# The gates' ring and the sums of quarters of h.T get memory of their own beside the projections of queries and keys, and the first sum is kept

## The chip, the core and the metric

The kernel runs as one program on one core of a Trainium2 chip. A core has a matrix engine (PE in the profile), three engines for elementwise work (DVE, ACT, POOL), a queue engine (SP) and 16 DMA engines, which share one on-chip memory; each engine works through its own instructions in a fixed order and waits for others by semaphores. The metric is the device time of one execution in microseconds. The kernel before was run three times: 1585.13, 1587.35 and 1588.13 us, so the median is 1587.35 us.

## What is computed

One layer of a decoder trunk: a token mixer with three branches (a gated short convolution, a state space model called S5, and latent attention), and then a mixture of experts. Sequence and model width are 1024. The change touches the mixer's input projection and its gates:

```python
proj = h @ w_in                              # 1024 x 1024 times 1024 x (2016 + 3 x 1024)
(xc, gc, gb, u_ssm, c_q, c_kv, k_r,
 g_conv, g_ssm, g_attn) = jnp.split(proj, IN_SPLITS, axis=-1)
y_conv = (gb * causal_conv(gc * xc)) @ w_up_conv
y_ssm  = s5_branch(u_ssm, ...) @ w_up_ssm
y_attn = attention(rms_norm(c_q), rms_norm(c_kv), k_r, ...) @ w_up_attn
merged = sigmoid(g_conv) * y_conv + sigmoid(g_ssm) * y_ssm + sigmoid(g_attn) * y_attn
y = merged @ w_o
```

## The kernel before

All matrix products take f32 operands as two parts each, a high part and a low one (`split_into`, L117 to L129: the cast that makes the high part runs on ACT at L125, the subtraction that leaves the low part on DVE at L129), and three matmuls replace one (`mm3`, L139 to L142, low times high first). The modulated input stands transposed on chip as eight pairs of tiles hh[k], hl[k] of 128 x 1024 ("h.T"). A block of 128 columns of `w_in` is a tile of 512 KB that SP loads (named raw), that is split into whi and wlo, and that gives 48 matmuls of 128 x 512 (`proj`, two halves of eight steps of three).

The mixer (`mixer`, L279) goes through these steps, and this is also the order in which they are written: the S5 branch up to its outputs; the first five of the eight gates of attention (`gates_att(0, GA, ...)` with GA = 5: projection, a sigmoid on ACT at L1075, a DMA to memory that ACT issues at L468); `proj_qkv` (L877), which projects c_q, c_kv and k_r into the tile cq and then normalises it by rows in a long chain of small operations on DVE (square L921, split L129, ones-matmul ps_ss L924 and L925 on PE, scale L927, `rsqrt` L145 to L153 with a square root on ACT at L148 and a reciprocal on DVE at L149, result L930), after which ACT issues one DMA of cq to memory, called cqd (L932, 1.5 MB); the last three gates of attention; `moving_sums`; `pairs`; and then `branches` (L1079), the up-projections of the convolution and of S5.

`pairs` computes 28 more blocks of `w_in` two at a time with seven products in place of eight (Strassen's scheme in Winograd's form, `pair_proj`, L365). For this h.T is cut into four quarters, and three sums of quarters (t2, t3, t4) are made once in `moving_sums` (L342 adds the two parts of a tile back together, L348 makes the sums, t0h to t2l are their two parts). A fourth, t1 = b12 - b11, is formed on the way to t2. It is dropped there, and within the first pair `moving_sum1` (L356) forms it anew (L360, L361) and splits it into the right halves of hh[0..3] and hl[0..3], which nothing needs whole any more. The same sums of quarters are made of every pair of weight tiles (L375, L379), and split into wsa (tiles sah and sal), w22 and wsb.

The order on each engine is fixed when the program is built. A scheduler takes the operations as they are written and moves one ahead of another where its own estimate says that the engine would else wait; memory decides what may move, since a tile of a pool that lies where a closed pool lay waits for the last use of what was there. Two pools matter. `qkv` holds all tiles of `proj_qkv`, cq among them. `stp` is opened after `qkv` is closed, in the same memory, and holds the ring of four tiles that the gates, the convolution's inputs and its outputs go round in, the split sums t0h to t2l, eight spare tiles, and the split sums of weights. So the ring's tile for the sixth gate, and the first part t0h, wait for `proj_qkv` to end and in part for the landing of cqd.

## Time and profile before

| | |
|---|---|
| three runs | 1585.13, 1587.35, 1588.13 us, median 1587.35 us |
| the profiled execution | 1582.0 us, of which the trace's span is 1579.9 us |
| PE busy in the span | 1419.6 us, 90% |
| DVE busy | 1196.8 us, 76% |
| ACT busy | 733.4 us, 46% |
| mean granted TensorE clock, of full speed | 0.954 |

A profile is taken of one execution. Its rows are in microseconds from the span's start. "Idle before" is the time for which an engine had nothing to run ahead of an instruction, and the arrow names the operation whose end released it. In the text, a gate or a pair is named by its place in the list above: the norm chain is the end of `proj_qkv`, the transition is the step from the last pair to `branches`.

### The profile page before, as it was taken

What the parts mean: (1) busy time and instruction counts of PE and PEld (TensorE: products, weight loads), DVE (VectorE), ACT (ScalarE), POOL (GpSimd) and SP (SyncE); (2) the same over time, 40 slices, a digit from 0 to 9 for tenths busy, and PEclk for the clock granted to TensorE, in tenths of its full rate; (3) what the DMA queues carried; (4) which work ended last, traced back from release to release, by engine and by line L of the source; (5) the groups of instructions that cost most, each with busy time, mean ns of one, the idle gap of its engine ahead of it and who ended that gap; (6) DMA issues with size and microseconds to landing.
All of it is one profiled execution on the core that took longest, in us unless ns stands there. A gap on an engine that the chain in (4) does not pass through costs nothing.

```text
span 1579.9 us, 20183 instructions
## 1 busy us (share of the span) xinstructions
PE 1419.6 (90%) x6996; PEld 1144.4 (72%) x6996; DVE 1196.8 (76%) x1861; ACT 733.4 (46%) x1192; POOL 442.5 (28%) x599
## 2 busy tenths in 40 slices
PE   5599799479999999999799979999979999999983
PEld 3477678368888887887588867788967888888841
DVE  8464687898775547756587788778887999999948
ACT  6232112242223334130477763335424998999853
POOL 7999930000000000006211252400322322222216
PEclk9799999799999999999799998999999999999977
DMA  9232221132122248968200035634623777777643
GB/s 382 80 113 88 73 58 27 67 101 97 56 107 107 107 145 308 326 161 224 36 15 12 4 114 192 225 133 151 251 79 115 303 282 287 289 297 272 255 182 146
DMA packets 79940, 247.50 MB, mean 157 GB/s; under 512 B 18460, under 2 KB 29780, under 8 KB 71000
## 3 DMA queue, kind: packets, MB, share of 16 engines
q1 hardware_dynamic: 53670, 200.47, 36.0%
q10 hardware_dynamic: 15218, 24.68, 4.5%
q0 software_dynamic: 10944, 20.99, 4.2%
q8 instruction: 56, 0.92, 0.2%
q14 instruction: 52, 0.43, 0.1%
HBM read 252.74 MB, written 55.10 MB: 195 GB/s over the span
## 4 chain that ended last, share of the span: by engine, by line
PE 58%; DVE 14%; POOL 12%; DMA 7%; issue 5%; ACT 3%; ACTq 0%; DVEq 0%; POOLq 0%; SPq 0%
PE ps_mm L140 9%; PE ps_mm L141 9%; PE ps_mm L142 9%; DMA yd<-y,idx 4%; PE ps_up L140 3%; PE ps_h L140 3%; PE ps_h L142 3%; PE ps_h L141 3%; PE ps_up L141 3%; PE ps_up L142 3%; PE ps_O L1272 2%; PE ps_T L1258 2%; PE ps_y L140 1%; PE ps_y L142 1%; PE ps_tr L1635 1%
## 5 line engine op out<-in xcount | busy, mean ns | idle before, releaser
L1138 POOL TENSOR_TENSOR mg<-mg,sg 128x512 f32<-128x512 f32 x16 | 23.5, 1476 | 496.4 <-DVE sg L1137 492.8
L140 PE MATMUL ps_mm<-hh,wlo 128*128 128x512 f32 x304 | 123.5, 406 | 22.7 <-ACT sg L1075 15.6
L142 PE MATMUL ps_mm<-hh,whi 128*128 128x512 f32 x304 | 123.1, 405 | 0.0
L141 PE MATMUL ps_mm<-hl,whi 128*128 128x512 f32 x304 | 122.7, 404 | 0.0
L125 ACT CAST whi<-raw 128x1024 fp32r<-128x1024 f32 (+1 forms) x45 | 46.8, 1040 | 134.0 <-PE ps_up L142 65.2
L1672 POOL DMA_INDIRECT yd<-y,idx x33 | 46.5, 1409 | 170.4 <-ACT y L1671 98.4
L140 PEld LDWEIGHTS ps_mm<-hh,wlo 128*128 128x128 f32 x304 | 58.7, 193 | 37.6 <-ACT sg L1075 16.1
L129 DVE TENSOR_TENSOR qh<-wo,qh 128x1024 fp32r<-128x1024 f32 x66 | 80.5, 1220 | 5.1 <-ACT qh L125 5.1
L129 DVE TENSOR_TENSOR ql<-wo,ql 128x1024 fp32r<-128x1024 f32 x66 | 79.5, 1219 | 4.8 <-ACT ql L125 4.8
L129 DVE TENSOR_TENSOR wlo<-raw,whi 128x1024 fp32r<-128x1024 f32 x44 | 60.4, 1373 | 26.5 <-ACT whi L125 26.5
L125 ACT CAST qh<-wo 128x1024 fp32r<-128x1024 f32 x66 | 70.0, 1061 | 4.1 <-DMA wo<-exp 4.1
L142 PEld LDWEIGHTS ps_mm<-hh,whi 128*128 128x128 f32 x304 | 58.6, 193 | 14.9 <-issue 1.0
L141 PEld LDWEIGHTS ps_mm<-hl,whi 128*128 128x128 f32 x304 | 58.8, 193 | 13.7 <-issue 0.2
L125 ACT CAST ql<-wo 128x1024 fp32r<-128x1024 f32 x66 | 68.2, 1052 | 0.0
L125 ACT CAST xh<-ps_tr 128x512 fp32r<-128x512 f32 x66 | 39.5, 599 | 55.5 <-PE ps_tr L1635 55.4
L1610 POOL DMA_INDIRECT xg<-h2d,idx x35 | 37.1, 1061 | 77.1 <-PE ps_tr L1635 63.5
L1244 DVE TENSOR_REDUCE sm<-ps_S 128x1 f32<-128x256 f32 (+3 forms) x64 | 49.2, 770 | 10.8 <-PE ps_S L1241 10.1
L129 DVE TENSOR_TENSOR pl<-ps_T,ph 128x512 fp32r<-128x512 f32 (+1 forms) x80 | 45.9, 581 | 14.0 <-ACT ph L125 12.6
L140 PE MATMUL ps_up<-ah,wlo 128*128 128x512 f32 x128 | 50.6, 403 | 5.1 <-ACT ah L125 2.9
L391 DVE TENSOR_TENSOR sp<-ps_mm,sp 128x512 f32<-128x512 f32 x48 | 32.8, 686 | 28.0 <-PE ps_mm L142 27.8
L1245 ACT ACTIVATE p<-ps_S,sm 128x256 f32<-128x256 f32 (+3 forms) x64 | 48.5, 758 | 10.0 <-DVE sm L1244 9.4
L140 PE MATMUL ps_mm<-wo,ml 128*128 128x512 f32 x128 | 50.0, 398 | 2.8 <-DVE sg L1354 2.8
(727 smaller groups left out, 4733.2 us busy)
## 6 DMA issues: line engine op xcount, KB each, us to landing
wo<-exp SPq DMA_DIRECT2D x111, 1024.0 KB
raw<-w_in SPq DMA_DIRECT2D x43, 512.0 KB
adr<-w_ada SPq DMA_DIRECT2D x32, 512.0 KB
wada<-w_ada SPq DMA_DIRECT2D x16, 512.0 KB
fy<-yd SPq DMA_DIRECT2D x16, 512.0 KB
sga<-sg ACTq DMA_DIRECT2D x8, 512.0 KB
sgc<-sg ACTq DMA_DIRECT2D x8, 512.0 KB
sgs<-sg ACTq DMA_DIRECT2D x8, 512.0 KB
```

The lines of the kernel that those rows point to most:

```text
L125: nc.scalar.copy(out=hi, in_=src)
L129: e.tensor_tensor(out=lo, in0=src, in1=hi.bitcast(F32), op=ALU.subtract)
L140: mm(ps, wl, xh, start=first, stop=False)
L141: mm(ps, wh, xl, start=False, stop=False)
L142: mm(ps, wh, xh, start=False, stop=last)
L391: v.tensor_tensor(out=out, in0=p, in1=x, op=op)
L1244: v.tensor_reduce(out=sm[:], in_=x, axis=AX.XY if two else AX.X, op=ALU.max, negate=True)
L1245: act.activation(out=y, in_=x, func=AF.Exp, bias=sm[:], accum_out=d)
L1258: pe.transpose(pt[:, k2 * 256 + qi * 128:k2 * 256 + qi * 128 + 128], prob[h, c, qi][:, ks], self.ident[:])
L1272: pe.matmul(po[:, 0:256], vv[:, kt, h].rearrange("p z d -> p (z d)"), x[z], start=kt == 0 and z == 0, stop=kt == 2 * c + 1 and z == 1)
L1610: self.nc.gpsimd.indirect_dma_start(out=self.xg[b % 2][:], out_offset=None, in_=self.h2d[:], in_offset=bass.IndirectOffsetOnAxis(ap=self.i ...
L1672: nc.gpsimd.indirect_dma_start(out=self.yd[:], in_=y[:], in_offset=None, out_offset=bass.IndirectOffsetOnAxis(ap=self.idx[:, 1, b:b + 1], ...
```

## The change

The ring becomes a pool of its own with two tiles, opened before S5 (it takes the place of the pool `sgp`, which held two gate tiles during S5). A pool `tsp` with the split sums and four more tiles that keep t1 is opened before `qkv`. `stp` is still opened after `qkv` in its memory; it now holds the convolution's weights, four spare tiles, the split sums of weights, and two tiles of their own for the convolution's outputs and for gc. `moving_sum1` no longer forms t1, and only splits the kept tiles. The four tiles that kept t1 serve afterwards as the scratch of `evac_b`.

```diff
@@ -282,8 +282,9 @@
         with ExitStack() as hs:
             hpool = hs.enter_context(tc.tile_pool(name="hpool", bufs=1, reuse_waits="tile"))
             self.hslot = lambda n, k, x="", dt=F32R: hpool.tile([128, S], dt, name=f"{n}{k}{x}", tag=f"{n}{k}")
+            ring = hs.enter_context(tc.tile_pool(name="ring", bufs=1, reuse_waits="tile"))
+            self.ring = lambda n: ring.tile([128, S + 2], F32, name=n, tag="ring", bufs=2)
             with ExitStack() as st:
-                self.sgp = st.enter_context(tc.tile_pool(name="sgp", bufs=1, reuse_waits="tile"))
                 self.s5p = st.enter_context(tc.tile_pool(name="s5p", bufs=1, reuse_waits="tile"))
                 self.banks_for(mm=4, a=2, b=2)
                 self.uses = {"ss": "ab"}
@@ -307,13 +308,13 @@
                             prep.append(self.s5_prep(q + 2))
                     if self.stop == "s5":
                         return False
-                    self.gates_att(0, GA, lambda: self.sgp.tile([128, S], F32, name="sg", tag="sg", bufs=2))
+                    self.gates_att(0, GA)
+            self.tsp = hs.enter_context(tc.tile_pool(name="tsp", bufs=1, reuse_waits="tile"))
             with tc.tile_pool(name="qkv", bufs=1, reuse_waits="tile") as self.qkv:
                 self.proj_qkv()
+            self.gates_att(GA, KT)
+            self.moving_sums()
             self.stp = hs.enter_context(tc.tile_pool(name="stp", bufs=1, reuse_waits="tile"))
-            self.ring = lambda n: self.stp.tile([128, S + 2], F32, name=n, tag="ring", bufs=4)
-            self.gates_att(GA, KT, lambda: self.ring("sg")[:, :S])
-            self.moving_sums()
             self.pairs()
         with ExitStack() as st:
             self.brp = st.enter_context(tc.tile_pool(name="brp", bufs=1, reuse_waits="tile"))
@@ -333,33 +334,29 @@
 
     def moving_sums(self):
 
-        v, P = self.nc.vector, self.stp
+        v, P = self.nc.vector, self.tsp
         raw = lambda: self.rawp.tile([128, 1024], F32, name="raw", tag="raw")
         parts = [[P.tile([128, 4, 512], F32R, name=f"t{i}{z}") for z in "hl"] for i in range(3)]
+        self.tmp = [P.tile([128, 512], F32, name=f"t1{k}")[:] for k in range(4)]
         for k in range(4):
             r = [raw(), raw()]
             for a in range(2):
                 v.tensor_tensor(out=r[a][:], in0=self.hh[4 * a + k][:].bitcast(F32),
                                 in1=self.hl[4 * a + k][:].bitcast(F32), op=ALU.add)
             b11, b12, b21, b22 = (r[a][:, n * 512:(n + 1) * 512] for a in range(2) for n in range(2))
-            t = [raw(), raw()]
-            t2, t3, t4, t1 = (t[i][:, n * 512:(n + 1) * 512] for i in range(2) for n in range(2))
+            t1, t = self.tmp[k], raw()
+            t2, t3, t4 = t[:, :512], t[:, 512:], b11
             for o, x, y in ((t1, b12, b11), (t2, b22, t1), (t3, b22, b12), (t4, t2, b21)):
                 v.tensor_tensor(out=o, in0=x, in1=y, op=ALU.subtract)
             for i, x in enumerate((t2, t3, t4)):
                 self.split_into(parts[i][0][:, k], parts[i][1][:, k], x)
         self.tq = [[[x[:, k] for k in range(4)] for x in p] for p in parts]
         self.t1 = None
-        self.spare = [P.tile([128, 512], F32, name=f"sp{i}")[:] for i in range(8)]
 
     def moving_sum1(self):
 
-        v = self.nc.vector
         for k in range(4):
-            x = self.rawp.tile([128, 1024], F32, name="raw", tag="raw")
-            v.tensor_tensor(out=x[:], in0=self.hh[k][:].bitcast(F32), in1=self.hl[k][:].bitcast(F32), op=ALU.add)
-            v.tensor_tensor(out=x[:, :512], in0=x[:, 512:], in1=x[:, :512], op=ALU.subtract)
-            self.split_into(self.hh[k][:, 512:], self.hl[k][:, 512:], x[:, :512])
+            self.split_into(self.hh[k][:, 512:], self.hl[k][:, 512:], self.tmp[k])
         self.t1 = self.quarter(0, 1)
 
     def pair_proj(self, ta, tb, evac):
@@ -389,7 +386,7 @@
 
         def tt(out, p, x, op=ALU.add):
             v.tensor_tensor(out=out, in0=p, in1=x, op=op)
-        p1, u2, u3, u4 = self.spare[:4]
+        p1, u2, u3, u4 = self.spare
         t2, t3, t4 = self.tq
         nc.scalar.copy(out=p1, in_=prod(w1, 0, self.quarter(0, 0)))
         p = prod(w1, 1, self.quarter(1, 0))
@@ -412,7 +409,8 @@
         v = nc.vector
         cw = P.tile([128, 4, 3], F32, name="cw")
         nc.scalar.dma_start(out=cw[:], in_=self.a["conv_w"])
-        ring = self.ring
+        self.spare = [P.tile([128, 512], F32, name=f"sp{i}")[:] for i in range(4)]
+        ring = lambda n: self.ring(n) if n[0] in "gs" and n != "gc" else P.tile([128, S], F32, name=n, tag="cv", bufs=2)
         half = lambda n: slice(n * 512, (n + 1) * 512)
         for t in (0, 2):
             gx = []
@@ -443,7 +441,7 @@
                 cv.append(c)
 
             def evac_b(b, n, write, cv=cv, t=t):
-                x = self.spare[4 + 2 * b + n]
+                x = self.tmp[2 * b + n]
                 write(x)
                 v.tensor_tensor(out=cv[b][:, half(n)], in0=cv[b][:, half(n)], in1=x, op=ALU.mult)
                 if n:
@@ -461,11 +459,11 @@
                         nc.scalar.dma_start(out=self.sgd[z][m + b], in_=sg[b])
                 self.pair_proj(t0 + m, t0 + m + 1, evac)
 
-    def gates_att(self, m0, m1, tile):
+    def gates_att(self, m0, m1):
 
         for m in range(m0, m1):
-            sg = self.gate(T_GA + m, tile())
-            self.nc.scalar.dma_start(out=self.sgd[2][m], in_=sg[:])
+            sg = self.gate(T_GA + m, self.ring("sg")[:, :S])
+            self.nc.scalar.dma_start(out=self.sgd[2][m], in_=sg)
 
     def ada_rest(self, i):
 
```

The change moves instructions on all engines; those of three are shown. A first place is the end of the norm chain on PE, where before two pairs of ones-matmuls (ps_ss) close the chain and the projection of the last gate follows; hh and whi are parts of h.T and of a weight tile, t0h and sah parts of the first sum of quarters and of the first sum of weights. Before:

```order
L141 MATMUL ps_mm<-hl_536,whi 128x512
L142 MATMUL ps_mm<-hh_535,whi 128x512
L924 MATMUL ps_ss<-ntl,oner 128x512
L925 MATMUL ps_ss<-nth,oner 128x512
L924 MATMUL ps_ss<-ntl,oner 128x512
L925 MATMUL ps_ss<-nth,oner 128x512
L140 MATMUL ps_mm<-hh_183,wlo 128x512
L141 MATMUL ps_mm<-hl_189,whi 128x512
L142 MATMUL ps_mm<-hh_183,whi 128x512
```

and now:

```order
L141 MATMUL ps_mm<-hl_536,whi 128x512
L142 MATMUL ps_mm<-hh_535,whi 128x512
L922 MATMUL ps_ss<-ntl,oner 128x512
L923 MATMUL ps_ss<-nth,oner 128x512
L922 MATMUL ps_ss<-ntl,oner 128x512
L923 MATMUL ps_ss<-nth,oner 128x512
L140 MATMUL ps_mm<-t0h,sal 128x512
L141 MATMUL ps_mm<-t0l,sah 128x512
L142 MATMUL ps_mm<-t0h,sah 128x512
```

All 72 matmuls that stood between the last ones-matmul and the first use of sal (48 of the last gate and 24 of the first pair's first two products) now stand ahead of the last ones-matmuls, and the first pair's third product follows them directly.

At the same place on ACT, around the DMA of cqd, before:

```order
L148 ACTIVATE nt_2302<-nt_2301 128x512
L148 ACTIVATE nt_2324<-nt_2323 128x512
L932 DMA cqd<-cq 128x3x1024
L1075 ACT_TABLE_LOAD
L1075 ACTIVATE sg<-ps_mm 128x512 x4
L125 CAST t0h<-raw 128x512
L125 CAST t1h<-raw 128x512
```

and now:

```order
L125 CAST nth<-nt_2317 128x512
L148 ACT_TABLE_LOAD
L148 ACTIVATE nt_2304<-nt_2303 128x512
L148 ACTIVATE nt_2326<-nt_2325 128x512
L930 DMA cqd<-cq 128x3x1024
L411 DMA cw<-conv_w 128x12
L125 CAST sah<-raw 128x1024
L125 CAST w22h<-raw 128x512
L125 CAST sbh<-raw 128x1024
L391 COPY sp_2594<-ps_mm 128x512
```

The sigmoids of the last gates and the casts of the sums have moved up between the square roots, a table load stands ahead of the last square roots, and the first instruction behind the DMA of cqd is the cast that makes sah.

The second place is the transition, where the last sigmoid of the last pair and its DMA (sgs) stand beside the first work of `branches`: the splits of the convolution's outputs (ah, al), the gelu of S5's outputs (cv) and its split (gh, gl). On ACT before:

```order
L459 ACTIVATE sg<-sg 128x512
L461 DMA sgs<-sg 128x1024
L125 CAST ah<-raw 128x1024 x4
L1102 ACT_TABLE_LOAD
L1102 ACTIVATE cv<-raw 128x1024 x2
L125 CAST whi<-raw 128x1024
L1102 ACTIVATE cv<-raw 128x1024 x2
```

and now:

```order
L457 ACTIVATE sg<-sg 128x512
L1100 ACT_TABLE_LOAD
L1100 ACTIVATE cv<-raw 128x1024 x2
L459 DMA sgs<-sg 128x1024
L125 CAST ah<-raw 128x1024 x4
L1100 ACTIVATE cv<-raw 128x1024
L125 CAST whi<-raw 128x1024
```

The table load and two gelus have moved ahead of the last DMA of sgs and of the four casts ah. On DVE before, from the last sum of the last pair (the first row):

```order
L391 TENSOR_TENSOR sg<-ps_mm,sp_2593 128x512
L129 TENSOR_TENSOR al<-raw,ah 128x1024 x4
L268 TENSOR_SCALAR aacc<-adr,cond 128x1024
L127 CAST gh<-cv 128x1024 x2
L270 SCALAR_TENSOR_TENSOR aacc<-adr,cond,aacc 128x1024
L129 TENSOR_TENSOR gl<-cv,gh 128x1024 x2
L270 SCALAR_TENSOR_TENSOR aacc<-adr,cond,aacc 128x1024
L1112 TENSOR_TENSOR mg_4493<-ps_up,sg 128x512 x2
```

and now:

```order
L388 TENSOR_TENSOR sg<-ps_mm,sp_2597 128x512
L127 CAST gh<-cv 128x1024
L268 TENSOR_SCALAR aacc<-adr,cond 128x1024
L127 CAST gh<-cv 128x1024
L129 TENSOR_TENSOR gl<-cv,gh 128x1024
L129 TENSOR_TENSOR al<-raw,ah 128x1024
L270 SCALAR_TENSOR_TENSOR aacc<-adr,cond,aacc 128x1024
L129 TENSOR_TENSOR gl<-cv,gh 128x1024
L129 TENSOR_TENSOR al<-raw,ah 128x1024 x3
L270 SCALAR_TENSOR_TENSOR aacc<-adr,cond,aacc 128x1024
```

Where four subtractions al stood first there now stand the two casts gh, a first part gl and a sum aacc (for the conditioning vector), and in the built program the second gh waits for the semaphore that the last DMA of sgs counts up; only behind it come the al.

## Rows read from the trace of the kernel before

**Rows 1.** Busy time by stretch: span, PE, PEld, DVE, ACT, POOL, clock, DMA, GB/s.

```profile
242.50:304.00 61.50, 43.65 (x187) 34.55 (x185) 57.17 (x73) 11.14 (x16) 0.00 (x0) 0.89 0.06 13
306.00:309.00 3.00, 2.54 (x6) 2.06 (x7) 0.00 (x0) 0.90 (x2) 0.00 (x0) 0.50 0.98 385
311.00:334.90 23.90, 17.07 (x63) 13.08 (x61) 22.07 (x33) 10.39 (x17) 0.00 (x0) 0.86 0.31 108
350.00:605.00 255.00, 253.64 (x1094) 205.09 (x1092) 168.53 (x220) 74.08 (x96) 0.00 (x0) 1.00 0.30 106
605.00:760.00 155.00, 148.69 (x661) 120.36 (x661) 103.58 (x109) 40.26 (x40) 29.99 (x26) 0.99 0.85 250
```

**Rows 2.** DVE in order of time, norm chain to first pair: start, us, operation.

```profile
242.51 1.28 DVE L897 TENSOR_TENSOR nt<-ps_mm,nt 64x512 f32<-64x512 f32 x2 [5.62 <-ACT nt L896]
...
303.25 0.75 DVE L930 SCALAR_TENSOR_TENSOR cq<-cq,gain,nt 128x512 f32<-128x512 f32 x1
311.02 0.69 DVE L129 TENSOR_TENSOR t0l<-raw,t0h 128x512 fp32r<-128x512 f32 x1 [7.01 <-ACT t0h L125]
...
330.88 3.49 DVE L360 TENSOR_TENSOR raw<-hh,hl 128x1024 f32<-128x1024 f32 x3
...
334.89 1.22 DVE L129 TENSOR_TENSOR sal<-raw,sah 128x1024 fp32r<-128x1024 f32 x1
```

**Rows 3.** The chain that ended last, between 255 and 350 us: start, us.

```profile
304.04 5.33 DMA cqd<-cq
```

**Rows 4.** PE in order of time, the same stretch.

```profile
306.46 0.80 PE L140 MATMUL ps_mm<-hh,wlo 128*128 128x512 f32 x1 [15.64 <-ACT sg L1075]
...
310.47 0.63 PE L140 MATMUL ps_mm<-hh,wlo 128*128 128x512 f32 x1
...
319.10 0.39 PE L140 MATMUL ps_mm<-hh,wlo 128*128 128x512 f32 x1
...
326.51 0.80 PE L140 MATMUL ps_mm<-hh,wlo 128*128 128x512 f32 x1 [6.56 <-DVE wlo L129]
...
336.16 0.50 PE L140 MATMUL ps_mm<-t0h,sal 128*128 128x512 f32 x1 [1.53 <-DVE sal L129]
```

**Rows 5.** ACT in order of time, the same stretch.

```profile
304.52 1.28 ACT L1075 ACT_TABLE_LOAD   x1 [9.21 <-DVE cq L930]
305.81 1.09 ACT L1075 ACTIVATE sg<-ps_mm 128x512 f32<-128x512 f32 x2
...
330.99 1.05 ACT L125 CAST sah<-raw 128x1024 fp32r<-128x1024 f32 x1 [2.51 <-DVE raw L375]
```

**Rows 6.** ACT and DVE in order of time, around a DMA of sgc.

```profile
527.35 0.33 ACTq L461 DMA_DIRECT2D sgc<-sg  x1
...
531.39 0.69 DVE L391 TENSOR_TENSOR sg<-ps_mm,sp 128x512 f32<-128x512 f32 x1 [2.62 <-PE ps_mm L142]
```

**Rows 7.** ACT's DMA queue, 526-531 and 612-614 us: packets, MB, share.

```profile
q10 hardware_dynamic: 288, 1.05, 52.5%
...
q10 hardware_dynamic: 1, 0.00, 0.0%
```

**Rows 8.** ACT in order of time, transition.

```profile
605.06 0.33 ACTq L461 DMA_DIRECT2D sgs<-sg  x1
...
609.39 1.28 ACT L1102 ACT_TABLE_LOAD   x1
610.69 4.02 ACT L1102 ACTIVATE cv<-raw 128x1024 f32<-128x1024 f32 x2
```

**Rows 9.** DVE in order of time, transition.

```profile
606.56 4.63 DVE L129 TENSOR_TENSOR al<-raw,ah 128x1024 fp32r<-128x1024 f32 x4 [2.19 <-ACT ah L125]
...
612.79 0.70 DVE L127 CAST gh<-cv 128x1024 fp32r<-128x1024 f32 x1 [0.93 <-ACT cv L1102]
```

**Rows 10.** Waits of PE behind it: total, times, longest.

```profile
PE ps_up L140 <- DVE sg L1137: 1.3, 1, 1.3
...
PE ps_S L140 <- DVE qf L1209: 3.8, 1, 3.8
```

## The prediction

> **What bounds the kernel now.** I read the busy time by stretch first. From 350 to 605 us, where the pairs run, PE is busy for 253.64 of 255.00 us at full clock, and DVE only for 168.53 [rows 1]: nothing that makes DVE's work there less can be seen in the time. From 605 to 760 us, in the branches, PE is busy for 148.69 of 155.00 us. So PE sets the time on both sides, and what is to be won or lost lies in the places where it stands still. In order of time there are three of them at the end of the norm chain: 15.64 us before 306.46, 6.56 us before 326.51 and 1.53 us before 336.16, which starts the first pair's third product [rows 4]. Behind that start PE runs on. The reader is to see who is late: DVE is busy for 57.17 of the 61.50 us from 242.50 to 304.00 [rows 1], ends its last L930 at 304.00, then stands for 7.01 us until t0h is there, and makes from 311.02 on what pair 0 needs [rows 2]. Between lies the landing of cqd, 5.33 us from 304.04 on, on the chain that ended last [rows 3], because the ring and the parts lie where cq lay. So here DVE is the limit, with a hole of 7 us in the middle of its work.
>
> **Part 1, the norm chain and the first pair.** The sums and their splits now lie in memory that is free, and stand ahead of the last L930. They fill DVE's holes, but they also push the end of the norm chain, and with it cqd, back. The new end of the chain, worked out from 242.5 on: DVE's own 57.2 us, plus its work from 311.0 to 334.9, 22.1 us [rows 1], less the three L360 that fall away there, 3.5 us [rows 2], less the split of w22 that now stands behind (0.7, like the split t0l of the same size [rows 2]), plus the four splits hl of the kept t1, which stood behind the third product and now stand ahead (4 x 0.7). That is 77.9 us, so 320.4 us if DVE never waits. The 4.3 us of waits that it has now between 242.5 and 304.0 may stay in part: 320.4 to 324.7; since so much more work is at hand, I take 321.0.
>
> What is left behind that end is a chain: cqd must land, since sah, sal and the other split sums of weights still lie in cq's memory (5.33 us, [rows 3]); then ACT casts sah (1.05, [rows 5]), DVE makes sal (1.22, and 0.05 to PE, from 334.89 to 336.16 [rows 2, 4]). 321.0 + 0.04 + 5.33 + 1.05 + 1.27 = 328.7 for the start of the third product, where 336.16 stood: 7.5 us less, with 3.8 and 8.1 as the ends.
>
> All other matmuls stand ahead of it now, so PE has one long pause in place of three. After the pauses of 15.64 and 6.56 us PE went on at the lower level: 0.50 of the clock, 1.2 GHz, from 306 to 309 us [rows 1]; after the one of 1.53 us it did not (0.50 us, against 0.80 for a first matmul after the long ones). So the third product now starts slowly, which it did not do before. The price: from 306.46 to 310.47 there are nine steps in 4.01 us, from 310.47 to 319.10 thirty-six in 8.63 us [rows 4], so 0.446 against 0.240, and nine times the difference is 1.9 us. Part 1 gives 7.5 - 1.9 = 5.6 us, with 2 (3.8 - 1.9) and 8 (no slow start) as bounds.
>
> The four adds L360 and four subtractions L361 that the kept t1 saves count no further: three L360 are in the sum above, the rest ran on DVE while PE had work. The sigmoids of the last gates now stand between the square roots, which costs four more table loads, 1.28 us each [rows 5]. ACT has room for them: it is busy for 11.14 us of those 61.50 [rows 1]. One is ahead of the last square roots; it needs no data and runs while DVE makes the reciprocal ahead, so I set it at nothing; with that cover gone it is 1.28 us.
>
> The Trainium skill speaks against this order: its page "ScalarE: Activation LUTs", in "What ACT_TABLE_LOAD costs", gives about 1.28 us for the load and about 1.38 us more for a drain, 2.66 us a switch, and its section "Table sets: the hidden batching unit" advises doing everything of one set before the next. The trace agrees on the load alone: it starts at 304.52 and lasts 1.28, and the sigmoid starts at 305.81, 0.01 us behind it [rows 5]; the same stands at the transition, 609.39 and 610.69 [rows 8]. By the page the sum at the end of this part would be 2.8 us higher (one drain at the last square roots, one at the transition).
>
> **Part 2, the pairs.** The removed work is DVE's, which has 86 us to spare there. The ring of two is the open point: a gate's tile is written again one pair later. The last DMA of sgc of a pair is issued at 527.35, the next write of its tile is at 531.39 [rows 6], 4.0 us later, and both DMAs of that pair, 1.05 MB, have moved by 531 [rows 7]. It fits, barely; and a late write would first use up PE's four banks of products (each product is twelve matmuls, 2.8 us). I set the part at 0.
>
> **Part 3, the transition.** Now ACT issues the last sgs at 605.06, and al's first split ends 1.16 us after 606.56, at 607.7 [rows 8, 9]; PE goes on with it. In the new order the table load and two gelus come first: 605.06 + 1.28 = 606.3, gelus of 2.01 each until 608.4 and 610.4 [rows 8]. The last sgs is issued behind them; ACT's queue may do that while the second gelu runs, at 608.4, or after it, at 610.4. The second gh waits for it to land, because gh lies where the ring lay. How long that takes is not shown for that time. Quietly, it took at most 3.7 us (527.35 to 531); at the transition, against SP's loads of w_ada, the queue was empty only by 612, 6.9 us after 605.06 [rows 7, 8]. The loads run into six tiles, and DVE frees none before the sums aacc, so three us later they are mostly done: I am nearer to the quiet row, 4.4 us. Then gh (0.7), gl and al (1.16 each, a quarter of the 4.63 for four al) stand behind one another on DVE: 3.0 us [rows 9]. So al's first split ends at 608.4 + 4.4 + 3.0 = 615.8, 8.1 us later than now; the ends are 608.4 + 3.7 + 3.0 = 615.1 (7.4 us) and 610.4 + 6.9 + 3.0 = 620.3 (12.6 us). PE has nothing else: the batch of 48 matmuls behind it passes all of it on.
>
> Some comes back, since DVE, POOL and the loads gain that time on PE: the wait of 1.3 us for sg (L1137) goes [rows 10]. Of the 3.8 us that PE later waits for qf [rows 10] none to all may go; I take 1.5, nearer to none, because DVE makes qf behind the same matmuls.
>
> **The sum.** -5.6 + 8.1 - 1.3 - 1.5 = -0.3 us. The profiled execution of before took 1582.0 us (span 1579.9), 5.3 us under the median of the three runs; I put the sum on both, so about 1581.7 for a profiled one and 1587.0 as median. A measurement of this kernel can tell about 0.2%, 3.2 us, from no change.
>
> **The rivals.**
> Faster: the transition is short. If the second gh doesn't have to wait for the sgs, because it has landed by the end of the second gelu, al ends at 610.4 + 3.0 = 613.4, 5.7 us later than now; with the whole 3.8 us of qf given back the sum is -5.6 + 5.7 - 1.3 - 3.8 = -5.0, 1582.3. For it: the transfer itself is half a megabyte, and ACT's queue may issue earlier than I think. Against it: 6.9 us in the only row at that place. It decides from 2.9 us under my sum: the landing alone can give 2.4, and qf the rest. 26%.
>
> Slower: the last sgs lands late. Issued after the second gelu and under the loads of w_ada, it holds the second gh, and all al behind it, until 617.3: 12.6 us, and the sum is -5.6 + 12.6 - 1.3 - 1.5 = +4.2, 1591.5; with DVE's waits in the norm chain unfilled (-2 in place of -5.6) 1595. For it: the queue was empty only by 612. Against it: it needs both ends at once. It decides from a landing 3.5 us later than I take. 14%.
>
> Slower, too: the ring of two stalls. At 6.9 us in place of 3.7 DVE's write waits 2.9 us at each of the seven steps from one pair of gates to the next, 20 us, 1607, if PE's banks didn't cover it; with three more banks to fill they cover over 2.9 us. 4%.
>
> The change doesn't do what it says: the gates and sums wait on after all. Then part 1 is 0 and the sum 8.1 - 1.3 - 1.5 = +5.3, 1592.6. The order on PE speaks against it: 72 matmuls have moved. 4%.
>
> My forecast, no difference that can be measured, has 52%; its own range is 1584.2 to 1590.5. With the faster case and part of the slower ones the range is 1581.5 to 1592.5. Faster by over 0.2%: 0.26; within: 0.52; slower: 0.22.
>
> **What would show it.** Right: in the changed profile DVE hardly waits between 242 and 320; L930 ends near 321; cqd's landing is the longest piece ahead of sah; the third product starts near 328.7 after a pause of over 10 us, at a clock of 0.50; the pairs keep PE at 99%; between the last ps_mm and the first al PE waits some 11 us in place of 3, for ah and then for al; and the second gh names sgs as its releaser. Wrong, if the third product starts before 326 or after 333, if the pairs show waits for sg, or if PE's waits at the transition are under 8 or over 15 us.

## The result: 0.7% slower, and the profile after

Five runs of the changed kernel had a median of 1597.83 us (1594.38 to 1600.88), five of the kernel before 1585.69 us (1585.13 to 1588.13). The ratio is 1.0074, with a 95% interval of 1.0056 to 1.0092: 12 us slower, and outside the range that was predicted. The profiled execution took 1599.46 us, its span 1597.6 us, at a mean clock of 0.949. Single executions of one kernel differ here by 3 to 12 us, so what a kernel takes is told by medians of several runs below, and a profile only tells where in the program the time lies.

Busy time by stretch in the changed kernel, with the columns of [rows 1]:

```profile
242.50:304.00 61.50, 57.70 (x237) 46.37 (x236) 57.69 (x81) 28.32 (x41) 0.00 (x0) 0.94 0.22 67
245.45:326.70 81.25, 60.41 (x244) 47.73 (x242) 78.10 (x107) 30.92 (x44) 0.00 (x0) 0.86 0.16 52
322.00:334.50 12.50, 0.09 (x1) 0.09 (x1) 5.92 (x10) 2.44 (x4) 0.00 (x0) 0.50 0.32 126
350.00:605.00 255.00, 254.70 (x1095) 205.59 (x1093) 163.27 (x212) 74.73 (x95) 0.00 (x0) 1.00 0.28 101
605.00:760.00 155.00, 142.45 (x620) 114.75 (x621) 98.57 (x105) 37.79 (x37) 22.25 (x20) 0.94 0.84 247
```

PE has much more to do in the norm chain than before (57.70 of 61.50 us, where 43.65 stood), and the pairs are full, at 254.70 of 255.00 us. What PE gained in the norm chain, it loses in one pause that ends at 334.41, and in the branches, where it was busy for 148.69 us of that stretch before [rows 1] and now for 142.45.

The start of the norm chain on ACT and DVE, in order of time (start, us, operation; in brackets the idle time before it and what ended it):

```profile
237.66 1.07 ACT L1049 COPY Y<-ps_ss 128x512 f32<-128x512 f32 x2 [5.90 <-PE ps_ss L1044]
244.31 0.48 ACTq L880 DMA_DIRECT2D ctab<-csd  x1
244.84 0.58 ACT L894 COPY nt<-ps_mm 64x512 f32<-64x512 f32 x1 [6.10 <-DMA ys<-Y]
245.45 1.28 DVE L895 TENSOR_TENSOR nt<-ps_mm,nt 64x512 f32<-64x512 f32 x2 [6.59 <-ACT nt L894]
```

the same place of S5 in the kernel before:

```profile
238.22 1.07 ACT L1051 COPY Y<-ps_ss 128x512 f32<-128x512 f32 x2 [4.51 <-PE ps_ss L1046]
```

and the chain's end now, from the chain that ended last (start, us, what):

```profile
309.88 0.62 ACT nth L125
310.51 1.28 ACT L148
311.81 0.64 ACT nt L148
...
325.91 0.76 DVE cq L928
326.69 5.34 DMA cqd<-cq
332.06 1.05 ACT sah L125
333.13 1.24 DVE sal L129
334.41 0.80 PE ps_mm L140
```

DVE starts the chain at 245.45, not at 242.51 [rows 2], because ACT stands ahead of it waiting for ys, S5's output, to land. Counted from S5's last copies into Y it is more: DVE starts 7.79 us behind them, where it was 4.29, so the wait grew by 3.5 us, and 0.6 of these are hidden because S5 ended earlier in this execution. DVE ends its last L928 (L930 before) at 326.66, and from there cqd, sah and sal follow one another as forecast. The third product of the first pair starts at 334.41; before, it started at 336.16 [rows 4].

The transition, ACT, DVE and PE in order of time, each apart:

```profile
606.11 1.28 ACT L1100 ACT_TABLE_LOAD   x1
606.12 0.33 ACTq L459 DMA_DIRECT2D sgs<-sg  x1
607.41 3.80 ACT L1100 ACTIVATE cv<-raw 128x1024 f32<-128x1024 f32 x2
611.11 3.87 ACT L125 CAST ah<-raw 128x1024 fp32r<-128x1024 f32 x4
```

```profile
609.36 0.69 DVE L127 CAST gh<-cv 128x1024 fp32r<-128x1024 f32 x1 [3.93 <-ACT cv L1100]
609.97 0.75 DVE L268 TENSOR_SCALAR aacc<-adr,cond 128x1024 f32<-128x1024 f32 x1
613.49 0.70 DVE L127 CAST gh<-cv 128x1024 fp32r<-128x1024 f32 x1 [2.77 <-DMA sgs<-sg]
614.10 1.22 DVE L129 TENSOR_TENSOR gl<-cv,gh 128x1024 fp32r<-128x1024 f32 x1
615.23 1.22 DVE L129 TENSOR_TENSOR al<-raw,ah 128x1024 fp32r<-128x1024 f32 x1
```

```profile
612.19 2.08 PE L140 MATMUL ps_up<-ah,wlo 128*128 128x512 f32 x4 [7.49 <-ACT ah L125]
616.50 0.79 PE L141 MATMUL ps_up<-al,whi 128*128 128x512 f32 x1 [2.23 <-DVE al L129]
```

The second gh names sgs as what it waited for, and the first al stands behind it and behind gl. PE waits 7.49 us for ah and 2.23 us for al.

Waits behind the transition, 605 to 772 us (waiting engine and tile, what it waited for: total, times, longest):

```profile
DVE aacc L270 <- DMA adr<-w_ada: 16.1, 5, 4.7
PE ps_mm L277 <- DVE aacc L270: 1.6, 1, 1.6
PE ps_up L140 <- DVE sg L1135: 1.5, 2, 1.1
```

and from 740 to 800 us:

```profile
DVE qf L1207 <- DMA tab<-csd: 5.8, 1, 5.8
PE ps_S L140 <- DVE qf L1207: 5.8, 1, 5.8
```

Neither wait of [rows 10] got shorter: that for sg is 1.5 us (1.3 before) and that for qf 5.8 us (3.8 before). New is that DVE stands five times for loads of w_ada, and that PE waits once for the sum aacc made of them.

To compare profiles, four starts on PE are used below: of the third product (first use of sal), of the last matmul of the pairs, of the first al, and of the first product of attention's scores (ps_S). In us from the span's start, with a second profile of the changed kernel (r1_after, below):

| | third product | last of the pairs | first al | first ps_S |
|---|---|---|---|---|
| before | 336.16 | 603.25 | 607.84 | 753.31 |
| changed | 334.41 | 604.31 | 616.50 | 765.85 |
| changed again | 333.53 | 603.31 | 615.37 | 763.80 |

So the changed kernel gains about 2 us ahead of the third product (1.2 to 1.4, counted from S5's last copies), has lost that by the end of the pairs, loses 7.5 at the transition (4.59 us from the last of the pairs to the first al before, 12.19 and 12.06 now) and 3 to 4 more by the first ps_S (145.47 us from the first al before, 149.35 and 148.43 now). By the first ps_S it is 12.5 us behind, in the second profile 10.5. From there to the end of the span the two profiles of the changed kernel take another 831.7 and 832.2 us, that of the kernel before 826.6, and those of the experiments 824.8 to 829.2. No experiment followed these 5 us, so whether they belong to the change stays open.

### The profile page after: what moved, and what is told of

It is laid out like the page before. It is cut to its first block, busy times and chain, and to the rows that moved or that the text cites. A ratio compares the mean times of both kernels' runs of the same rounds, so it can differ in the third digit from the quotient of the medians.

```text
span 1597.6 us, 20194 instructions
## 1 busy us (share of the span) xinstructions
PE 1425.5 (89%) x6996; PEld 1146.1 (72%) x6996; DVE 1192.4 (75%) x1853; ACT 738.2 (46%) x1196; POOL 440.9 (28%) x599
## 4 chain that ended last, share of the span: by engine, by line
PE 54%; POOL 12%; DVE 12%; DMA 11%; issue 7%; ACT 3%; ACTq 0%; SPq 0%; POOLq 0%; DVEq 0%
PE ps_mm L140 10%; PE ps_mm L141 9%; PE ps_mm L142 9%; DMA yd<-y,idx 5%; PE ps_up L141 2%; PE ps_up L142 2%; PE ps_up L140 2%; PE ps_h L140 2%; PE ps_h L142 2%; PE ps_h L141 2%; DMA adr<-w_ada 2%; PE ps_O L1270 2%; PE ps_T L1256 2%; PE ps_S L140 1%; PE ps_S L142 1%
## 5 line engine op out<-in xcount | busy, mean ns | idle before, releaser
L141 PE MATMUL ps_up<-al,whi 128*128 128x512 f32 x128 | 51.5, 403 | 2.2 <-DVE al L129 2.2
L1256 PE MATMUL ps_T<-ident,p 128*128 128x128 f32 x288 | 49.4, 281 | 2.7 <-ACT p L1243 1.9
```

Source lines behind the costliest of these rows:

```text
L141: mm(ps, wh, xl, start=False, stop=False)
L1256: pe.transpose(pt[:, k2 * 256 + qi * 128:k2 * 256 + qi * 128 + 128], prob[h, c, qi][:, ks], self.ident[:])
```

## The experiments

Every kernel computes the whole reference. Each ratio is to the kernel before, timed in the same session. Four theories were at stake: that the order at the transition costs the time; that the wait for ys at the start of the norm chain does; that the wait for cqd at its end does; and that the kept sum gives nothing.

**a1_order.** The changed kernel with the transition's order of before. `issue_after(x)` tells the scheduler that what stands under it is not moved ahead of x; hi_i and lo_i are the last of the casts ah and of the subtractions al.

```diff
         for t in range(4):
-            self.split_into(ah[t], al[t], self.load(self.cvd[t])[:])
+            raw = self.load(self.cvd[t])
+            hi_i = nc.scalar.copy(out=ah[t], in_=raw[:])
+            lo_i = v.tensor_tensor(out=al[t], in0=raw[:], in1=ah[t].bitcast(F32), op=ALU.subtract)
...
             if m % 2 == 0:
-                gelu(m // 2)
+                with self.tc.issue_after(hi_i), self.tc.issue_after(lo_i):
+                    gelu(m // 2)
```

Expected:

> The changed kernel with the transition's order put back: on ACT the casts ah stand ahead of the table load and the gelus, on DVE the al ahead of gh; nothing else is edited, and the memory stays as in the change. If the loss is the transition and what hangs behind it (first al 7.6 us later after the last pair's matmul, then 4 us in the branches and 2 at the start of attention), the first al comes some 4.6 us after the last ps_mm and the median falls from 1597.8 to about 1584 to 1587. If the order of the loads of w_ada is a loss of its own, only the 7.6 us come back, about 1590. If the loss sits in the ring of two tiles or in the norm chain, it stays near 1597.

Measured: 1586.86 us (12 runs, 1580.49 to 1589.12), ratio 1.0013 [1.0000, 1.0027]. From the last of the pairs to the first al it is 7.74 us, in place of 12. Two sums aacc had still slipped in ahead of al, one of which waits for a load (DVE in order of time):

```profile
604.57 0.74 DVE L268 TENSOR_SCALAR aacc<-adr,cond 128x1024 f32<-128x1024 f32 x1
608.80 1.28 DVE L270 SCALAR_TENSOR_TENSOR aacc<-adr,cond,aacc 128x1024 f32<-128x1024 f32 x1 [3.48 <-DMA adr<-w_ada]
610.00 2.35 DVE L1094 TENSOR_TENSOR al<-raw,ah 128x1024 fp32r<-128x1024 f32 x2
```

With only the order changed, most of the loss is gone, the part behind the transition with it: from the first al to the first ps_S it takes 144.37 us.

**a2_ctab.** In the changed kernel the pool `qkv` lies at bytes 149152 and up, and its first tile ctab (to 153248) lies over S5's last tile Y (150048 to 154144), whose DMA to ys must have landed before ctab may be loaded. ACT issues that load, ahead of the first copy of the chain. Here the tiles nth and ntl are made first, so that ctab lies behind Y; the order on all engines stays that of the changed kernel. The edit has a second effect: cq, too, moves up by 8 KB, so that the split sums sah and sal don't lie over it any more (the subject of a3_stp). So the run tests both places together.

```diff
+        pre = {x: [half(x, F32R) for _ in range(2)] for x in ("nth", "ntl")}
         ctab = self.qkv.tile([128, S], F32, name="ctab")
...
-                    sh, sl_ = (half(x, F32R) for x in ("nth", "ntl"))
+                    sh, sl_ = (pre[x].pop(0) if pre[x] else half(x, F32R) for x in ("nth", "ntl"))
```

Expected:

> The changed kernel with the pool qkv laid out in another order, so that the table ctab no longer lies over S5's last tile Y (whose DMA ys it waits for now), and sah and sal no longer lie over cq. If the place of ctab made the norm chain start 2.9 us late, L895 on DVE starts near 242.5 again in place of 245.4, the last L928 ends near 323.7, and sah no longer waits for cqd, so the third product starts near 325 to 327 in place of 334.4; the time falls by 7 to 9 us to about 1590, since the transition is untouched. Rival: PE had been late for other reasons (DVE's length of work), then the third product starts no earlier than 331 and the time falls by under 4 us.

Measured: 1588.25 us (12 runs, 1581.29 to 1593.37), ratio 1.0035 [1.0020, 1.0050]. ACT and DVE in order of time:

```profile
236.65 1.07 ACT L1050 COPY Y<-ps_ss 128x512 f32<-128x512 f32 x2 [5.90 <-PE ps_ss L1045]
240.96 1.28 DVE L896 TENSOR_TENSOR nt<-ps_mm,nt 64x512 f32<-64x512 f32 x2 [2.35 <-ACT nt L895]
322.47 1.04 ACT L125 CAST sah<-raw 128x1024 fp32r<-128x1024 f32 x1 [9.69 <-DVE cq L929]
```

ACT's wait for ys falls from 6.10 to 2.61 us, and DVE starts the chain 4.31 us behind S5's last copies, as before; and sah waits for DVE, no longer for cqd. The profile is of this kernel's fastest run, 7 us under its median; in it the third product starts at 324.83. By the medians about half of the loss is gone, 5 to 6 us, for both places together; what ctab's place alone costs in the whole was not measured. In this profile PE stands at the transition as long as in the changed kernel (11.98 us to the first al), but from there to the first ps_S it takes only 144.25 us: with the same order and everything 8 to 9 us earlier, PE stands 0.13 us for the sums aacc.

**a3_stp.** Of the tiles of `stp`, sah (157408 to 161504 in the changed kernel) reaches 64 bytes into cq, which begins at 161440, and sal lies wholly over it. Here cw and the spare tiles, 8 KB, get a pool `spp` of their own behind `stp`, which moves sah and sal out of cq.

```diff
+            self.spp = hs.enter_context(tc.tile_pool(name="spp", bufs=1, reuse_waits="tile"))
             self.pairs()
...
-        cw = P.tile([128, 4, 3], F32, name="cw")
+        cw = self.spp.tile([128, 4, 3], F32, name="cw")
...
-        self.spare = [P.tile([128, 512], F32, name=f"sp{i}")[:] for i in range(4)]
+        self.spare = [self.spp.tile([128, 512], F32, name=f"sp{i}")[:] for i in range(4)]
```

Expected:

> The changed kernel with the spare tiles in a pool behind the split sums of weights, so that sah and sal lie over ctab and the norm's first scratch, not over cq; ctab stays where the change put it. If only the landing of cqd holds the third product, it starts right behind the last L928 and sal, at about 328 in place of 334.4, and the time falls by some 6 us to about 1592; if it is held by DVE's own work as well, sal comes no earlier than 331 and the time by under 4 us.

Measured: 1584.27 us (12 runs, 1579.79 to 1587.60), ratio 0.9998 [0.9985, 1.0012]. ACT in order of time:

```profile
325.18 0.38 ACTq L931 DMA_DIRECT2D cqd<-cq  x1
325.59 0.50 ACTq L412 DMA_DIRECT2D cw<-conv_w  x1
326.13 1.04 ACT L125 CAST sah<-raw 128x1024 fp32r<-128x1024 f32 x1 [9.69 <-DVE cq L929]
330.54 0.62 ACT L125 CAST w22h<-raw 128x512 fp32r<-128x512 f32 x1 [3.36 <-DMA cqd<-cq]
```

sah starts 0.95 us behind the issue of cqd, in place of 5.37 in the changed kernel (326.69 and 332.06), and the third product at 328.49. Only w22h still waits for the landing, and PE has the third product to do meanwhile. The whole loss is gone, although the transition is as it was (11.89 us): the pairs end 7 to 8 us earlier, and the branches take 144.94 us to the first ps_S. Not all of that is the landing. With the split sums of weights in their new place the matmuls of the pairs also follow one another faster (a9_shift): from the third product to the last of the pairs it takes 267.42 us, against 269.90 and 269.78 in the changed kernel, which is 2.4 us of the 7 to 8. And in the branches the built program isn't in the order of the changed kernel: some loads, splits and sums aacc have changed places, so the 144.94 us don't tell the memory from the order.

**k1_keep.** The kernel before, with the kept t1 alone, in four of its spare tiles.

```diff
-            t = [raw(), raw()]
-            t2, t3, t4, t1 = (t[i][:, n * 512:(n + 1) * 512] for i in range(2) for n in range(2))
+            t1, t = self.spare[4 + k], raw()
+            t2, t3, t4 = t[:, :512], t[:, 512:], b11
```

Expected:

> The kernel before with nothing but the first sum t1 kept (in four of the spare tiles that lie idle until evac_b), in the memory of before. It takes the four L360 and four L361 off DVE. By the rows of before at most the 1.53 us of waiting ahead of the third product can go: 1584 to 1586. If the scheduler moves more for it, the time may go either way by some us, and the trace shows where.

Measured: 1584.53 us (12 runs, 1580.44 to 1588.93), ratio 1.0003 [0.9989, 1.0017]. In the old memory the kept sum is worth nothing that can be measured.

**r1_after.** The changed kernel again, unedited, in the session of the next three.

Expected:

> The changed kernel once more, unedited, on the chip and beside the runs of the kernel before that the next three are compared with. A ratio near 1.0074 again (12 us) makes the differences to the earlier experiments sound; and the second profile tells whether the 4 us in the branches and 3 us at the start of attention belong to the change (then first al to first ps_S takes 149 us again, and PE waits 1.6 us for aacc) or to that one execution (then about 144 to 145, as in the three experiments).

Measured: 1592.46 us (6 runs, 1591.27 to 1597.90), ratio 1.0066 [1.0051, 1.0080]. Its profile is in the table above.

**a7_order_stp.** Both repairs in the changed kernel: a3's pool, and a1's order with the sums aacc behind al, too.

```diff
             if m % 2:
-                self.ada_rest(next(steps))
+                with self.tc.issue_after(lo_i):
+                    self.ada_rest(next(steps))
```

Expected:

> The changed kernel with both repairs: the transition's order put back on ACT and DVE (the sums aacc behind the al, too), and sah and sal out of cq's memory. If the norm chain's gain and the transition's loss simply add, the third product starts near 328.5, the last pair ends about 596, the first al follows 4.6 us behind it, and the time is 7 us under that of the kernel before: about 1577, ratio 0.9955. If the gain is given back later (loads of w_ada, start of attention), the ratio stays at 0.999 to 1.0, as it is for the second repair alone.

Measured: 1574.29 us (6 runs, 1573.10 to 1575.64), ratio 0.9953 [0.9938, 0.9967]: 7 us faster than the kernel before. At the end of the norm chain sah starts 0.95 us behind the issue of cqd, as in a3. PE at the transition, in order of time:

```profile
598.60 1.95 PE L140 MATMUL ps_up<-ah,wlo 128*128 128x512 f32 x4 [2.94 <-ACT ah L1094]
600.35 0.63 PE L141 MATMUL ps_up<-al,whi 128*128 128x512 f32 x1
```

PE doesn't wait for al any more, and stands for 2.94 us where it stood for 9.72.

**b2_gelu_first.** The kernel before, with the order of the change at the transition: two gelus and their splits ahead of ah and al (act is the second gelu, sub its subtraction).

```diff
+        act, sub = [[getattr(x, "ins", x) for x in gelu(t)] for t in range(2)][1]
+        with self.tc.issue_after(act), self.tc.issue_after(sub):
+            for t in range(4):
+                self.split_into(ah[t], al[t], raws[t][:])
```

Expected:

> The opposite test: the kernel before in its memory, with nothing but the transition's order of the change put in (table load and two gelus ahead of the casts ah on ACT, two gh and gl ahead of the al on DVE). If that order is the loss, the first al comes some 10 to 13 us after the last ps_mm in place of 4.6, and the time rises by 6 to 9 us, to about 1592 (ratio 1.004 to 1.006). If the loss needs the new memory, or hides behind the loads, it rises by under 3 us.

Measured: 1600.57 us (6 runs, 1597.11 to 1603.01), ratio 1.0118 [1.0100, 1.0135]. The order alone, in the old memory, costs more than the whole change. But it is harsher than the change's own, since both gh and gl, and then the split of the weights, stand ahead of PE's first product (PE in order of time):

```profile
602.14 0.40 PE L142 MATMUL ps_mm<-hh,sbh 128*128 128x512 f32 x1
619.90 0.79 PE L140 MATMUL ps_up<-ah,wlo 128*128 128x512 f32 x1 [17.36 <-DVE wlo L129]
```

It is 18.35 us to the first al here, and 12 in the changed kernel. The run shows that such an order is paid in full, not what the change's own costs.

**k2_nokeep.** The changed kernel, with t1 formed anew in `moving_sum1` as before (`self.hh[k] + self.hl[k]`, then the difference of its halves).

Expected:

> The changed kernel with the first sum formed anew as before (four L360 and four L361 back on DVE, more raw tiles), the new memory kept. If the kept sum is what pays, the third product comes later and the time is 3 us and more over the changed kernel's; if it doesn't matter beside the memory, the time is that of the changed kernel within 2 us.

Measured: 1594.83 us (6 runs, 1593.02 to 1605.48), ratio 1.0095 [1.0070, 1.0120], against 1.0066 of the changed kernel beside it. The third product starts at 338.76, 5.2 us behind that of r1_after (4.7, counted from S5's last copies): the extra adds and subtractions stand ahead of the last L930, on an engine that has no room there. The intervals overlap, so the 0.3% are not shown by the medians alone, nor by the profiles: at the first ps_S this one is 3.0 us behind that of r1_after, and as a whole it is the shorter of the two (1594.17 and 1597.90 us). That the kept sum brings the third product forward is shown, what it is worth in the end is not. From the first al, at 621.11, to the first ps_S it takes 145.73 us here, with the transition as long as in the changed kernel (12.02 us).

**a8_all.** a7 with the repair of a2. No edit beyond these.

Expected:

> Three repairs together: the transition's order, sah and sal out of cq's memory, and ctab away from S5's last tile Y. If the late start of the norm chain (about 3 us) is on the path, the third product starts near 324 in place of 327.7, the last pair ends 3 to 4 us earlier than with two repairs, and the ratio to the kernel before falls from 0.9953 to about 0.993. Rival: the pairs or the loads behind them take it up, and the ratio stays at 0.995.

Measured: 1576.57 us (6 runs, 1573.78 to 1579.59), ratio 0.9945 [0.9924, 0.9965], not to be told from a7. The wait for ys is short as in a2 (ACT 2.62 us), but ACT now waits at the other end:

```profile
323.69 0.38 ACTq L932 DMA_DIRECT2D cqd<-cq  x1
329.10 0.35 ACTq L412 DMA_DIRECT2D cw<-conv_w  x1
329.49 1.05 ACT L125 CAST sah<-raw 128x1024 fp32r<-128x1024 f32 x1 [14.53 <-DMA cqd<-cq]
```

With nth and ntl first, cq lies at 169632 to 181920, and cw, the first tile of `spp` at 177824, now lies over it. So the load of 6 KB of convolution weights waits until cqd has landed, 5.4 us, and the cast that makes sah stands behind it on ACT. The third product starts at 331.85, 4.2 us behind that of a7; but S5's last copies are 3.4 us later in this execution (239.09 against 235.71), so only 0.8 us of that are the kernel's.

**a9_shift.** a7 with cw back ahead of the split weight sums, which moves these by 64 bytes and leaves the order on all engines as in a7.

```diff
-        cw = self.spp.tile([128, 4, 3], F32, name="cw")
+        cw = P.tile([128, 4, 3], F32, name="cw")
```

Expected:

> The kernel with two repairs, in the same order of instructions on every engine, with the split sums of weights 64 bytes further on (the small tile of the convolution's weights lies ahead of them). In that kernel a matmul of the pairs came every 0.2305 us, in the kernel before every 0.2320, in the changed one every 0.2328. If the place of the weights within their memory sets this, the shift brings back about 0.2326 and 2.5 us (ratio 0.997); if it is something else (the place of the spare tiles, which stays), the step stays at 0.2305 and the ratio at 0.9953.

Measured: 1579.03 us (12 runs, 1573.49 to 1583.73), ratio 0.9970 [0.9955, 0.9985]. The profile is of this kernel's fastest run, 5.5 us under its median. The third product starts at 327.54 (a7: 327.67). What differs is the step of a matmul in the pairs, the mean distance of the starts of two 128x512 matmuls that follow one another: 0.2328 us, as in the changed kernel, against 0.2305 in a7. For the some 1,176 matmuls of the pairs that would be 2.7 us, and the ratios' difference, 0.17%, is 2.7 us. But the two intervals overlap, and in the profiles the pairs take only 1.8 us longer from the third product on (269.36 against 267.59 us), of which 0.5 are left at the first ps_S. So the steps are plain, and what they are worth in the whole is not settled.

The two tiles for the convolution's outputs move with the sums, so the steps were also taken apart by the matmul's weights: with sah, sal and the two parts of w22 they are 0.227 to 0.228 us in a7 and 0.233 to 0.234 in a9, with sbh and sbl 0.233 to 0.234 in a7 and 0.232 in a9, and with whi and wlo, which didn't move, 0.232 to 0.233 in both. It is the products of the sums that moved.

**a10_order2.** The changed kernel with the order of a7 alone.

Expected:

> The changed kernel with the transition's order alone put back, this time with the sums aacc behind the al as well, as in the kernel before. If the transition costs 7.5 us and its echo in the branches 3 us, the first al comes 4.6 us after the last ps_mm, PE waits for no aacc, and the ratio falls from 1.007 to 0.999 to 1.001: the gain of the norm chain is then what is left to find. If the first of the two order repairs had already got it all, it stays at 1.0013.

Measured: 1583.02 us (12 runs, 1580.30 to 1587.25), ratio 0.9991 [0.9977, 1.0005]. It takes 4.60 us from the last of the pairs to the first al, and 144.81 from there to the first ps_S: with the order alone, both losses behind the pairs are gone. Beside a9, in the same session, it also prices the wait for cqd: up to the branches the two have the same order on every engine, and in the pairs the same step (0.2328 to 0.2329 us), but here sah and sal lie over cq. The medians are 1583.02 and 1579.03 us, 4.0 us apart, though the two intervals overlap a little.

**a11_cw.** a8 with cw in the pool `tsp`, as a tile of 128 bytes (everything behind it moves by that much).

```diff
-        cw = self.spp.tile([128, 4, 3], F32, name="cw")
+        cw = self.tsp.tile([128, 32], F32, name="cw")[:, :12].rearrange("p (t k) -> p t k", k=3)
```

Expected:

> All three repairs, and the convolution's weights cw moved out of the pool behind the split weight sums into the pool of the sums of quarters, so that their load needn't wait for the landing of cqd, behind which the cast that makes sah stood in the kernel with three repairs (cw issued at 329.10, 5.4 us behind cqd at 323.69; sah at 329.49). First theory (that wait ate what the table's repair gave): cqd, sah and sal follow one another without a gap, the third product comes about 4.9 us earlier against the end of the norm chain (3.4 us behind the issue of cqd instead of 8.2), and the ratio to the kernel before falls from 0.9945 to about 0.9915 (0.9900 to 0.9930). Rival (another wait has become the bound behind the norm chain, the loads of weights or the matmuls' own work): the third product comes earlier, but the ratio stays at 0.994 to 0.996. Beside it: everything in the memory of the projections and behind it moves by 128 bytes instead of the 64 of the shifted kernel; if only odd multiples of 64 cost, the matmul step in the pairs stays at 0.2303 us, if any move costs, it is 0.2326.

Measured: 1573.53 us (6 runs, 1569.04 to 1575.09), ratio 0.9927 [0.9906, 0.9948], the lowest of all. ACT in order of time:

```profile
324.66 0.38 ACTq L932 DMA_DIRECT2D cqd<-cq  x1
325.08 1.04 ACT L125 CAST sah<-raw 128x1024 fp32r<-128x1024 f32 x1 [9.15 <-DVE cq L930]
326.03 0.61 ACT L125 CAST w22h<-raw 128x512 fp32r<-128x512 f32 x1
```

The third product starts at 327.44, 2.78 us behind the issue of cqd, where it took 8.16 in a8. So the wait of cw is what a8 lost at that place. The median fell as the first theory said, but the interval reaches into what the rival allowed, so the medians alone don't settle it. The step came out at 0.2316 us, between the two that were named (which in the count used here are 0.2305 and 0.2328): which places are dear is not settled.

## Why the prediction was wrong

**The start of the norm chain** is the first step that failed: "the new end of the chain, worked out from 242.5 on". The sum of DVE's work was right (77.9 us predicted, 78.10 busy from 245.45 to 326.70). But the chain began 2.9 us later (3.5, counted from S5's last copies), since the new pools moved `qkv` so that ctab lay over a tile whose DMA had yet to land. Of the tiles that moved I had followed those that the change names, not the one whose load heads the chain. a2_ctab shows that place, where the 3.5 us are gone; its price in the whole is not shown by itself, since that run also frees sah and sal.

**DVE's waits** were taken at 0.6 us (321.0 against 320.4), within bounds of 0 and 4.3; they were 3.1. These are waits for ACT (1.08 us, for the square root behind the table load), PE (1.00) and the load of gain (0.79), which the added work did not fill. The table load that "I set at nothing" was on the chain, 1.28 us at 310.51 in the rows above; DVE stood 1.08 us for what came behind it. The square root starts 0.02 us behind its end, so a load costs ACT 1.28 us here. The Trainium skill's page "ScalarE: Activation LUTs" gives, in "What ACT_TABLE_LOAD costs", 1.38 us more for a drain; no row here shows one. The section "Table sets: the hidden batching unit" of the same page of the Trainium skill advises all of one set before the next, and was right in this: the mixed order was paid with one load on the path. With 2.9 and 2.5 us, and 0.2 for the work, the end came at 326.66 instead of 321.0. cqd, sah and sal behind it took what was forecast, and the third product started at 334.41 instead of 328.7, outside the bounds of the step.

**The cover of cqd's landing.** That sah and sal had to wait for it was in the sum, as a fact of the layout. For sah it was one by 64 bytes alone, but sal lay wholly over cq and would have had to wait without these. a3_stp shows what it was worth: sah starts 4.4 us sooner behind the issue of cqd, the third product 5.0 to 5.9 us earlier, and the kernel is at par with the one before, in part by the shorter step; a10 and a9 put the landing alone at 4.0 us.

**The slow start** was right: the third product starts at 0.50 of the clock, at the lower level, after a pause of 21.69 us. From there to the end of the pairs it takes 269.90 us, against 267.09 before. 1.9 of these 2.8 us were in the sum for the slow start; the mean step of a matmul in the pairs (a9_shift), 0.2328 us against 0.2320, makes the other 0.9 over 1,176 steps. So part 1 came out at +0.1 to +1.1 us by the end of the pairs, instead of -5.6.

**The pairs** were right: full, with no wait for sg, so the rival of a stalling ring fell.

**The transition** was right in size, 7.5 us instead of 8.1, by other pieces. sgs was issued at 606.12, during the table load, 2.3 us earlier than I had put it, and took 7.27 us to land, not the 4.4 that I took from the quiet row. The two errors nearly cancel: landed at 613.39, where 612.8 was predicted.

**The recovery** is the second step that failed, in its sign. -1.3 and -1.5 us were to come back in the branches; 3 to 4 us more were lost. The reason given, that DVE, POOL and the loads gain that time on PE, leaves out that the loads wait for DVE: a tile for w_ada is free when its sum aacc is made, and these sums now stood behind the same late splits. So the loads came as late as the splits, two of them on the chain that ended last:

```profile
661.20 14.85 DMA adr<-w_ada
...
732.87 15.41 DMA adr<-w_ada
```

Where the time went can be read on PE. It stands for the sum that the first of these loads ends in, and soon behind it the granted clock is at the lower of its two levels, 1.2 GHz (PE in order of time; busy time by stretch, columns as in [rows 1]):

```profile
677.48 1.28 PE L277 MATMUL ps_mm<-ones,aacc 128*128 128x1 f32 x10 [1.62 <-DVE aacc L270]
```

```profile
680.00:682.00 2.00, 2.00 (x6) 1.57 (x5) 0.96 (x1) 0.00 (x0) 0.00 (x0) 0.50 1.03 420
616.50:626.50 10.00, 10.00 (x33) 7.96 (x34) 10.00 (x10) 1.98 (x1) 0.00 (x0) 0.74 1.03 412
```

From 679.92 on seven matmuls come 0.43 us apart, in place of 0.23: 1.4 us. And in the first 10 us behind the first al PE gets through 33 matmuls at a clock of 0.74, where it was 36 at 0.83 before: 0.7 us. With the wait of 1.6 us that is 3.7 of the 3.9 us by which the stretch grew. The prediction put a price on a slow start in part 1 alone; behind the pause of some 11 us that it forecast for the transition it put none, and gave no reason.

a10_order2 shows that the loss goes with the order (144.81 us from al to ps_S). a2_ctab and k2_nokeep have the order of the changed kernel at the transition and are without most of it, too (144.25 and 145.73 us): PE stands for the same sum for 0.13 and 0.77 us there, and the clock doesn't fall behind it. In a2 everything is 8 to 9 us earlier than in the changed kernel, in k2 some 5 us later, so being early is not what decides. The sum comes just in time or just too late; why the load landed late in both profiles of the changed kernel is not shown. And qf, of which a part was to come back, is held by a load (tab), not by DVE's work ahead of it: 4.5 to 4.8 us of wait in a1, a2, a3, a7, a10 and b2, whichever order stands at the transition.

**The rivals and chances.** The slower rival was a late sgs; the transition did not decide, the two failed steps did, 6 us each. The late ctab and the late loads came from one omission, to follow what is freed late; DVE's waits and the clock did not. The 22% for slower were too few for a change that moves four pools.

What stays open: how the loss of the changed kernel adds up from its parts. The order repaired alone brings 0.75%, the memory alone 0.68%, both together 1.13% (1.0066 to 0.9953). Part of each is the loss in the branches, which either gives back; the split of that part was not measured by itself. In the memory's part, and in that of both, is also the shorter step in the pairs, up to 0.17% (a7 and a9). And the 5 us behind the scores that both profiles of the changed kernel show are not explained.

## What to carry to other kernels

When a pool moves, list for every tile on the chain that bounds the stage, loads included, which bytes it now shares with what, and when that is freed; an overlap with a tile that is still being written out, 64 bytes of one new tile and the whole of the next, cost 4 to 5 us here, and the small load of weights in a8 as much again. Filler work may fill an engine's holes, but each piece of it that the scheduler puts ahead of the split that the matrix engine waits for is paid in full; force that split to the front, as a7 did. Don't count on a stall being given back later: of the 7.5 us at the transition at most 1.2 came back by the first ps_S (a2), and in both profiles of the changed kernel 3 to 4 more were lost. And a pause of the matrix engine is to be charged with the slow start behind it, wherever the trace shows one.

## What was not expected of the hardware

The step of a 128x512 matmul in the pairs hangs on where the split weight sums lie: 0.2305 us in a3, a7 and a8, where they start at the beginning of their pool, 0.2328 in a9, 64 bytes on and in the same order, 0.2316 in a11, and 0.2320 in the kernel before. That is up to 1%, 1.8 to 2.7 us in the pairs. The changed kernel (in both profiles), a1, a2, a10 and k2, which have the sums at one and the same place, all show 0.2328 to 0.2329. The mechanism was not looked into.

A DMA of 512 KB took 7.27 us from issue to landing at the transition, under a DMA share of 0.94 from 605 to 622 us; in the pairs of the kernel before the prediction's row had it at 3.7 us at most, at a share of 0.47 from 527.35 to 531 us.
